# Feed-forward product stage: the activation remainders move from GpSimd to VectorE, the products are reordered, and split weights of three chunks are kept in DRAM

## The chip, the cores and the metric

The kernel runs on one core of a Trainium2 chip. The time is that of one execution in device microseconds (us). The engines are TensorE (PE: matmuls; PEld: its weight loads), VectorE (DVE), ScalarE (ACT), GpSimd (POOL) and the DMA queues, the main one of which is issued by SyncE (SP). Each engine works through its own instructions in the order of the program and waits for the others on semaphores.

## The reference

One step of a one-layer decoder: 2048 prompt tokens and 64 sample tokens of width 1024. The change touches only the second half of the feed-forward part:

```python
hid = jnp.square(jax.nn.relu(jnp.einsum('btd,df->btf', x, w_ff1)))     # 1024 -> 4096
x = _layer_norm(ALPHA * x + jnp.einsum('btf,fd->btd', hid, w_ff2), ln2_g, ln2_b)   # 4096 -> 1024
```

All is float32. The kernel gets near that accuracy from fp32r matmuls: each operand is cut in two, a rounded part and the remainder, and three products are summed (rounded x rounded, rounded x remainder, remainder x rounded).

## The kernel before

The prompt is worked on in four blocks of 512 tokens; block two (`b == 1`, the source counts from 0) also carries the 64 sample rows. Each block has four stages: the mixer (projections, recurrence, convolution), the output projection with layer norm, `ff1` (32 feature tiles against `w_ff1`) and `ff2`. The texts below number the blocks one to four.

**ff2.** The 4096 hidden features are eight chunks of 512 features (`NCH`; in block four the eighth chunk is worked off apart, after the other seven). For each chunk, tokens, features and output columns are halved, and a Strassen-like scheme does seven products in place of eight. A product (`step`) runs over all chunks before the next begins, so a block has 7 x 8 = 56 units, numbered here n = 0 to 55. A unit is 12 matmuls of 128x512 (L236 to L238). In block two the units of four of the steps (B11, B21, T1 and B22, the names in `SAMPLE`) carry four more, for the sample rows. A unit needs one weight tile of 128x1024 and one hidden tile of 128x512, each in two parts:

- the weight: SP loads it into one of three `st` buffers (L173); ACT rounds it into `wh` (L194); DVE subtracts and writes the remainder `wl` (L201). There are four `wh` and four `wl`. The call `weights(i)` prepares the unit three ahead, so `wh` of unit n+3 is written when TensorE has finished unit n-1. The steps T1 to T4 use sums of weight quarters, which DMAs of the POOL queue put together in DRAM in block one (`make_sums`).
- the hidden tile: `prepare` (L1033) works two units ahead. ACT rounds into `h` (L1040), and GpSimd writes the remainder `l` (L1041); three buffers each. Three of the steps also need a difference of hidden quarters, on DVE, in place (L1045, L1047, L1049); these were done at once, a unit after the use of the quarter that they overwrite, eight in a row.

**The products' banks.** Each product adds into two of the PSUM tiles named A to D (`PRODUCTS`). When its last chunk is done, DVE adds the two banks into the token rows `x1` (L1069, L1072: two instructions a destination, for T3 four); at the four sample steps it adds sample rows too (`sample_sums`, two or four instructions).

**Order on DVE.** What must wait for ACT is put into the list `later` and issued by the next `flush`, which `weights` calls first. So the program order on DVE after the last unit of a product is: the bank additions, then the weight remainder of the unit three ahead, then what `prepare` and the others left.

**The next block's input** comes as four tiles of transposed tokens (five for block two), put among the weights at `X_PLACES` and split in the same way. `tok` is a ring of eight 128x1024 tiles; four (five in block two) hold the rows `x1`.

Of the kernel before, what the change touches and what calls it, by code (L numbers as in the profile page):

```python
# [9 lines left out]
F32 = mybir.dt.float32  # L10
# [25 lines left out]
RAW = {"B11": 0, "B21": 1, "B12": 2, "B22": 3}  # L36
SUMS = ("T1", "T2", "T3", "T4")

PRODUCTS = (("B21", "C"), ("B11", "A"), ("T4", "D"), ("T2", "A"), ("T1", "B"), ("B22", "B"), ("T3", "A"))

SLOT_OF = {"B21": 3, "B11": 1, "T4": 2, "T2": 2, "T1": 1, "B22": 3, "T3": 0}

# [3 lines left out]

SAMPLE = {"B21": (1, ((0, 1),)), "B11": (0, ((0, 1), (1, -1))), "T1": (0, ((1, 1),)), "B22": (1, ((1, 1),))}

X_PLACES = (("B21", 2), ("B21", 5), ("B11", 2), ("B11", 5), ("B22", 5))
M_ORDER = (4, 5, 6, 7, 0, 1, 2, 3)  # L50


# [1 line left out]
def hybrid_step(ctx, tc, a, o):  # L54
# [10 lines left out]
    def new(shape, tag, bufs, dt=F32, of=None):  # L65
        count[0] += 1
        return (of or pool).tile(list(shape), dt, tag=tag, bufs=bufs, name=f"{tag}{count[0]}")
# [19 lines left out]
    def TOK(dt=F32):  # L87
        return new((P, D), "tok", 8, dt)
# [76 lines left out]

    def unit_dma():
        src, _, cols, _, _ = units[at["dma"]]
        st = TOK() if at["dma"] < 6 else new((P, D), "st", 3)
        if at["dma"] < 2:
            for half in (slice(0, D // 2), slice(D // 2, D)):  # L170
                nc.sync.dma_start(st[:, half], src[:, half])
        else:
            nc.sync.dma_start(st[:, :cols], src)  # L173
        stages[at["dma"]] = st
        at["dma"] += 1

    def unit_split():
        i = at["split"]
        at["split"] += 1
        _, scale, _, use, spare = units[i]  # L180
        st = stages.pop(i)
        if use is not None:
            use(st)
            return
        wh = new((P, D), "wh", 4, F32R)
        if i == 0:
            wl = new((P, D), "wl", 4, F32R)
            for half in (slice(0, D // 2), slice(D // 2, D)):
                split(wh[:, half], wl[:, half], st[:, half])
                flush()  # L190
            handles[i] = (wh, wl)
            return
        if scale is None:
            s.activation(wh, st, AF.Copy)  # L194
        else:
            s.activation(wh, st, AF.Identity, scale=scale)

        def low():
            wl = TOK(F32R) if spare else new((P, D), "wl", 4, F32R)
            if scale is None:  # L200
                v.tensor_tensor(wl, st, wh.bitcast(F32), ALU.subtract)  # L201
            else:
                v.scalar_tensor_tensor(wl, st, scale, wh.bitcast(F32), ALU.mult, ALU.subtract)
            handles[i] = (wh, wl)

        later.append(low)
# [10 lines left out]
    def weights(i, kept=0):  # L217

        ahead(i + 4 - kept)
        return handles.pop(i)  # L220
# [100 lines left out]
    def make_sums():  # L321
        def at(c, k):
            return a["w_ff2"][c * 4 + RAW[k]] if k in RAW else sums[c][k]

        for to, of, acc in (("T1", "B11", False), ("T3", "B22", False), ("T1", "B12", True), ("T3", "B12", True),
                            ("T2", "T3", False), ("T2", "B11", True), ("T4", "T2", False), ("T4", "B21", True)):
            for c in range(NCH):
                if acc:
                    g.dma_start(at(c, to), at(c, of), accum_op=ALU.add, max_dma_last_dim=4096)
                else:  # L330
                    g.dma_start(at(c, to), at(c, of), max_dma_last_dim=4096)
                yield

    making = make_sums()

    for b in range(NB):
        pl = {}
        pl["m1"] = [w_in(0)]
        if b == 0:
            for src, cols, use in x_units(0):  # L340
                add_unit(src, cols=cols, use=use)
        pl["m1"] += [w_in(i) for i in (4, 1, 5, 2, 6, 3, 7)]
        pl["m2"] = [w_in(20 + i) for i in range(8)]
        pl["m3"] = [[w_in(8 + 3 * ct + j) for j in range(3)] for ct in range(4)]
        pl["tiles"] = [[0, 1], [2, 3, 4] if b == SB else [2, 3]]

        pl["m4"] = [[(m, add_unit(a["w_out"][m], scale=onorm[:, m:m + 1] if m < 4 else None)) for m in ms]
                    for ms in (M_ORDER, M_ORDER[:-2])]
        nf = 8
        pl["f0"] = [[(f, add_unit(a["w_ff1"][f])) for f in fs] for fs in (range(nf), range(nf - 2))]  # L350
        pl["ff1"] = [(f, add_unit(a["w_ff1"][f])) for f in range(nf, NF)]
        pl["ff2"] = []
        pl["nc"] = NCH - 1 if b == NB - 1 else NCH
        nx = x_units(b + 1) if b + 1 < NB else []
        for step, _ in PRODUCTS:
            for c in range(pl["nc"]):
                pl["ff2"].append((step, c, add_unit(a["w_ff2"][c * 4 + RAW[step]] if step in RAW else sums[c][step])))
                if (step, c) in X_PLACES and nx:
                    src, cols, use = nx.pop(0)
                    add_unit(src, cols=cols, use=use)  # L360
        pl["last"] = [add_unit(a["w_ff2"][(NCH - 1) * 4 + k], spare=k == 3) for k in range(4)] if b == NB - 1 else []
        for src, cols, use in nx:
            add_unit(src, cols=cols, use=use)
        plan.append(pl)
# [7 lines left out]
    for b in range(NB):  # L372
# [451 lines left out]

        for i, _ in enumerate(main()):
            rec_step()
            if b == 0 and i >= 4:
                next(making, 0)
                next(making, 0)
            if i >= 16 and i % (3 if samp else 4) == 0:  # L830
                rec_step()
            if i % 2 == 0:
                pump()
# [199 lines left out]
        def prepare():  # L1033
            if not queue:
                return
            step, c = queue.pop(0)
            r = raw[c]
            x = r[:, SLOT_OF[step]]
            h, l = F((P, 2, 256), "h", 3, F32R), F((P, 2, 256), "l", 3, F32R)
            s.activation(h, x, AF.Copy)  # L1040
            g.tensor_tensor(l, x, h.bitcast(F32), ALU.subtract)  # L1041
            hid[step, c] = (h, l)

            if step == "T4":
                later.append(lambda: v.scalar_tensor_tensor(x, r[:, 0], -1.0, x, ALU.mult, ALU.subtract))  # L1045
            elif step == "T2":
                later.append(lambda: v.scalar_tensor_tensor(r[:, 1], x, -1.0, r[:, 1], ALU.mult, ALU.subtract))  # L1047
            elif step == "T1":
                later.append(lambda: v.scalar_tensor_tensor(r[:, 3], r[:, 2], -1.0, r[:, 3], ALU.mult, ALU.subtract))  # L1049
            elif step == "T3":  # L1050
                del raw[c]

        for i, (f, u) in enumerate(pl["ff1"]):
            if i >= len(pl["ff1"]) - 2:
                prepare()
            ff1(f, weights(u), segs)
        drain()
        norm_weights(1)
        if b == 0:
            for _ in making:  # L1060
                pass

        touched = set()

# [31 lines left out]
        to = dict(PRODUCTS)  # L1096
        banks = {}
        sample_rows()
        for step, c, u in pl["ff2"]:
            w = weights(u)  # L1100
            parts = [tuple(x[:, q * 512:q * 512 + 512] for x in w) for q in range(2)]
            prepare()
            if step in SAMPLE:
                sample_rows()
            if step == "T3" and pl["last"] and 2 <= c < 6:
                if c == 2:
                    last = [F((P, 4, 2, 256), "raw", NCH, F32R) for _ in range(2)]
                split(last[0][:, c - 2], last[1][:, c - 2], raw[NCH - 1][:, c - 2])
            k = to[step]
            first = k not in banks  # L1110
            if first:
                banks[k] = [PS() for _ in range(2)]
            h, l = hid.pop((step, c))
            for p in range(2):
                cs = slice(p * P, p * P + P)
                for q, (rh, rl) in enumerate(parts):
                    mm3_on(banks[k][p], h[:, q, cs], l[:, q, cs], rh, rl, first and q == 0, c == ncs - 1 and q == 1)
            if samp and step in SAMPLE:
                if c == 0:
                    ys = PS()  # L1120
                hp = spairs.pop(0)
                for q, (rh, rl) in enumerate(parts):
                    mm_pair(ys, hp[:, q, :], rh, rl, c == 0 and q == 0, c == ncs - 1 and q == 1)
            if c == ncs - 1:
                for t0, dh, sign in INTO[k][step]:
                    for p in range(2):
                        add_to(t0 + p, dh, banks[k][p], sign)
                if samp and step in SAMPLE:
                    sample_sums(ys, SAMPLE[step][1])
# [138 lines left out]
```

## Time and profile before

| | us |
|---|---|
| three timed runs | 2446.64, 2449.08, 2449.68 (median 2449.08) |
| profiled execution: its time | 2449.19 |
| profiled execution: its span, first to last instruction | 2447.4 |
| DVE busy / ACT busy / POOL busy | 1542.2 / 1114.9 / 524.9 |
| mean granted TensorE clock | 0.996 |

In the windows of the profile, "busy" of PE counts a matmul from its start to its modelled end; a matmul of 128x512 lasts 0.39 us but the next can start 0.227 us after it, so a busy PE can still be slower than it could be. In the rows of the waits, the three numbers are the sum in us, the count and the longest.

### The profile page before, as it was taken

The numbers are of one execution on the slowest core, as the hardware profiler recorded it, in microseconds if no ns is written. First come the engines' busy times: TensorE is split into PE (matmuls) and PEld (weight loads), VectorE is DVE, ScalarE is ACT, GpSimd is POOL, SyncE is SP. The second block draws the span as 40 slices with busy tenths as digits, with TensorE's granted clock in tenths as the row PEclk, the third lists the DMA queues.
The fourth block names the chain that finished last, engine by engine and source line by source line (L and its number), as shares of the span: only waits on it lengthen the run. The fifth ranks groups of instructions, "written<-read, shape, count | busy, mean of one in ns | idle before, by whom it ended". The sixth has DMA issues, their size and how long they took to land. (4 is left out here: it accounts for less than half of the span.)

```text
span 2447.4 us, 32997 instructions
## 1 busy us (share of the span) xinstructions
PE 2400.3 (98%) x12876; PEld 2051.5 (84%) x12876; DVE 1542.2 (63%) x2153; ACT 1114.9 (46%) x1794; POOL 524.9 (21%) x376
## 2 busy tenths in 40 slices
PE   7999999999999999999999999999999999999998
PEld 5888988878889889998778888988878888988876
DVE  5756822696865684227968857623886865822597
ACT  4334534654324354445554244534654334543553
POOL 3210000654001110004750000001662001000554
PEclk9999999999999999999999999999999999999999
DMA  9985423655223633225543225423654324433453
GB/s 329 277 233 174 160 97 112 199 186 179 79 78 75 211 121 104 87 96 164 180 149 118 91 80 190 144 96 129 206 188 146 104 82 159 161 103 116 163 184 113
DMA packets 103548, 358.79 MB, mean 147 GB/s; under 512 B 11552, under 2 KB 16032, under 8 KB 103392
## 3 DMA queue, kind: packets, MB, share of 16 engines
q1 hardware_dynamic: 91216, 313.88, 38.6%
q0 software_dynamic: 12032, 42.54, 6.5%
q8 instruction: 101, 1.65, 0.3%
q14 instruction: 55, 0.45, 0.1%
q10 hardware_dynamic: 144, 0.26, 0.0%
HBM read 345.59 MB, written 44.60 MB: 159 GB/s over the span
## 5 line engine op out<-in xcount | busy, mean ns | idle before, releaser
L201 DVE TENSOR_TENSOR wl<-st,wh 128x1024 fp32r<-128x1024 f32 x514 | 679.5, 1325 | 548.3 <-ACT wh L194 547.5
L230 PE MATMUL ps<-X,wh 128*128 128x512 f32 (+2 forms) x2272 | 779.6, 343 | 14.2 <-ACT X L155 11.0
L232 PE MATMUL ps<-X,wl 128*128 128x512 f32 (+2 forms) x2272 | 769.4, 339 | 1.0 <-DVE wl L201 1.0
L231 PE MATMUL ps<-X,wh 128*128 128x512 f32 (+2 forms) x2272 | 769.4, 339 | 0.5 <-DVE X L156 0.5
L194 ACT ACTIVATE wh<-st 128x1024 fp32r<-128x1024 f32 x515 | 543.1, 1055 | 381.0 <-DMA st<-T 90.8
L1041 POOL TENSOR_TENSOR l<-raw,h 128x512 fp32r<-128x512 f32 x217 | 391.6, 1808 | 947.3 <-ACT h L1040 930.9
L230 PEld LDWEIGHTS ps<-X,wh 128*128 128x128 f32 x2272 | 431.6, 190 | 60.6 <-ACT X L155 13.0
L232 PEld LDWEIGHTS ps<-X,wl 128*128 128x128 f32 x2272 | 431.3, 190 | 43.7 <-DVE wl L201 1.9
L231 PEld LDWEIGHTS ps<-X,wh 128*128 128x128 f32 x2272 | 431.7, 190 | 42.1 <-DVE X L156 2.6
L238 PE MATMUL ps<-wh,l 128*128 128x512 f32 x868 | 342.1, 394 | 8.9 <-POOL l L1041 8.9
L236 PE MATMUL ps<-wh,h 128*128 128x512 f32 x868 | 339.1, 391 | 6.3 <-DVE tok L1072 5.0
L237 PE MATMUL ps<-wl,h 128*128 128x512 f32 x868 | 339.2, 391 | 1.6 <-DVE wl L201 1.6
L1008 ACT ACTIVATE raw<-ps 128x256 f32<-128x256 f32 (+1 forms) x184 | 85.7, 466 | 372.6 <-PE ps L232 370.9
L238 PEld LDWEIGHTS ps<-wh,l 128*128 128x128 f32 x868 | 163.3, 188 | 53.1 <-POOL l L1041 19.9
L236 PEld LDWEIGHTS ps<-wh,h 128*128 128x128 f32 x868 | 163.4, 188 | 40.7 <-issue 6.2
L237 PEld LDWEIGHTS ps<-wl,h 128*128 128x128 f32 x868 | 163.2, 188 | 37.4 <-DVE wl L201 3.3
L1040 ACT ACTIVATE h<-raw 128x512 fp32r<-128x512 f32 x217 | 133.5, 615 | 7.7 <-PE ps L237 5.7
L262 POOL TENSOR_TENSOR sm<-sm,nhalf 128x1 f32<-128x1 f32 (+1 forms) x34 | 36.5, 1075 | 383.4 <-DVE sm L261 383.4
L230 PE MATMUL ps<-wh,X 128*128 128x512 f32 x256 | 104.0, 406 | 0.0
L230 PE MATMUL ps<-wh,S 128*128 128x512 f32 x256 | 101.3, 396 | 0.0
L232 PE MATMUL ps<-wh,X 128*128 128x512 f32 x256 | 100.3, 392 | 0.0
L232 PE MATMUL ps<-wh,S 128*128 128x512 f32 x256 | 99.9, 390 | 0.0
(204 smaller groups left out, 2560.4 us busy)
## 6 DMA issues: line engine op xcount, KB each, us to landing
st<-in_w_ff SPq DMA_DIRECT2D x249, 512.0 KB, 3.3
st<-T SPq DMA_DIRECT2D x124, 512.0 KB, 3.3
st<-in_w_in SPq DMA_DIRECT2D x110, 512.0 KB, 3.3
st<-in_w_out SPq DMA_DIRECT2D x56, 512.0 KB, 4.3
T<-in_w_ff POOLq DMA_DIRECT2D x48, 512.0 KB, 19.7
T<-T POOLq DMA_DIRECT2D x16, 512.0 KB, 17.8
lnb<-in_lnb SPq DMA_DIRECT2D x16, 512.0 KB, 5.9
tok<-in_x SPq DMA_DIRECT2D x16, 512.0 KB, 6.9
```

What stands on the lines that cost most here:

```text
L194: s.activation(wh, st, AF.Copy)
L201: v.tensor_tensor(wl, st, wh.bitcast(F32), ALU.subtract)
L230: te.matmul(out, lh, rh, start=first, stop=False)
L231: te.matmul(out, lh, rl, start=False, stop=False)
L232: te.matmul(out, ll, rh, start=False, stop=last)
L236: te.matmul(out, lh, rh, start=first, stop=False, skip_group_check=True)
L237: te.matmul(out, lh, rl, start=False, stop=False, skip_group_check=True)
L238: te.matmul(out, ll, rh, start=False, stop=last, skip_group_check=True)
L262: g.tensor_tensor(st[:n, 15:16], st[:n, 14:15], nhalf[:n, 0:1], ALU.pow)
L1008: s.activation(r[:, h0:h1], ps[:, :256 * (h1 - h0)].rearrange("p (s t) -> p s t", t=256), AF.Relu)
L1040: s.activation(h, x, AF.Copy)
L1041: g.tensor_tensor(l, x, h.bitcast(F32), ALU.subtract)
```

## The change

Six edits go together:

1. `prepare` calls `split`: the remainder `l` is a VectorE subtraction, put into `later`, in place of a GpSimd one issued at once.
2. The products run in the order T4, B11, B21, T2, T1, T3, B22. Their banks are then D, A, C, A, B, A, B; before they were C, A, D, A, B, B, A.
3. The differences of hidden quarters are no longer tied to `prepare`: `sum_rows` hands out one at a time, two in three units, from n = 3 to n = 37.
4. The tiles of the next block's input move from B21 and B11 (the first 16 units) to T3 and B22 (the last 16).
5. While `ff1` of block one runs, `keep_parts` makes the two parts of the weights of chunks 1, 4 and 6 for all seven steps: 21 tiles are loaded by SP, rounded by ACT, subtracted by DVE and stored as two tiles each by the POOL queue (42 stores). From block two on, those 3 of 8 units load both parts from DRAM straight into `wh` and `wl`; they have no `st` buffer, no rounding and no subtraction.
6. `make_sums` starts four steps later in the program and is finished ahead of `ff1`.

```diff
-PRODUCTS = (("B21", "C"), ("B11", "A"), ("T4", "D"), ("T2", "A"), ("T1", "B"), ("B22", "B"), ("T3", "A"))
+PRODUCTS = (("T4", "D"), ("B11", "A"), ("B21", "C"), ("T2", "A"), ("T1", "B"), ("T3", "A"), ("B22", "B"))
...
-X_PLACES = (("B21", 2), ("B21", 5), ("B11", 2), ("B11", 5), ("B22", 5))
+X_PLACES = (("T3", 0), ("T3", 4), ("B22", 0), ("B22", 3), ("B22", 5))
+KEPT = (1, 4, 6)
...
     def unit_dma():
         src, _, cols, _, _ = units[at["dma"]]
+        if isinstance(src, tuple):
+            at["dma"] += 1
+            return
...
     def unit_split():
...
+        if isinstance(src, tuple):
+            handles[i] = new((P, D), "wh", 4, F32R), new((P, D), "wl", 4, F32R)
+            for x, y in zip(handles[i], src):
+                nc.sync.dma_start(x.bitcast(F32), y)
+            return
...
+    def keep_parts():
+        last = None
+        for k, c in parts2:
+            t = TOK()
+            nc.sync.dma_start(t, quarter2(c, k))
+            if last:
+                last()
+            def done(t=t, to=parts2[k, c]):
+                h = TOK(F32R)
+                s.activation(h, t, AF.Copy)
+                def low():
+                    v.tensor_tensor(t.bitcast(F32R), t, h.bitcast(F32), ALU.subtract)
+                    g.dma_start(to[0], h.bitcast(F32))
+                    g.dma_start(to[1], t)
+                later.append(low)
+            last = done
+            yield
+        last()
...
-            if b == 0 and i >= 4:
+            if b == 0 and i >= 8:
                 next(making, 0)
...
-            s.activation(h, x, AF.Copy)
-            g.tensor_tensor(l, x, h.bitcast(F32), ALU.subtract)
+            split(h, l, x)
...
+        sumq = [(k, c) for k in ("T2", "T1", "B22") for c in range(ncs)]
+        def sum_rows():
...
+            later.append(lambda: v.scalar_tensor_tensor(r[:, to], r[:, of], -1.0, r[:, less], ALU.mult, ALU.subtract))
...
             ff1(f, weights(u), segs)
+            if b == 0:
+                next(keeping, 0)
...
-        for step, c, u in pl["ff2"]:
+        for n_, (step, c, u) in enumerate(pl["ff2"]):
             w = weights(u)
+            while (len(summed) * 3 + 6) // 2 <= n_ and sumq:
+                sum_rows()
...
             prepare()
```

On VectorE, at the end of the second product of block one, the rows were these (`tok` here are the token rows `x1`, `ps` the banks, `raw` the hidden quarters):

```order
L201 TENSOR_TENSOR wl_3899<-st_3879,wh_3881 128x1024
L1045 SCALAR_TENSOR_TENSOR raw_2149<-raw_2149 128x512
L1069 TENSOR_TENSOR tok_1929<-tok_1929,ps_3744 128x512
L1069 TENSOR_TENSOR tok_1931<-tok_1931,ps_3745 128x512
L201 TENSOR_TENSOR wl_3924<-st_3902,wh_3904 128x1024
L1045 SCALAR_TENSOR_TENSOR raw_2311<-raw_2311 128x512
L201 TENSOR_TENSOR wl_3949<-st_3927,wh_3929 128x1024
```

At the end of the first product of block one, VectorE's rows of the changed kernel are these (L1124 are the bank additions, L211 the weight remainders, L1101 the differences of hidden quarters, L158 the hidden remainders):

```order
L158 TENSOR_TENSOR l_3875<-raw_2191,h_3874 128x512
L1124 SCALAR_TENSOR_TENSOR tok_1818<-tok_1818,ps_3741 128x512
L1124 SCALAR_TENSOR_TENSOR tok_1820<-tok_1820,ps_3742 128x512
L211 TENSOR_TENSOR wl_3914<-st_3893,wh_3895 128x1024
L1101 SCALAR_TENSOR_TENSOR raw_2934<-raw_2934 128x512
L158 TENSOR_TENSOR l_3898<-raw_2353,h_3897 128x512
L211 TENSOR_TENSOR wl_3939<-st_3918,wh_3920 128x1024
```

The hidden remainder of the second unit after the product's end (`l_3898`) now stands on VectorE behind the two bank additions, the weight remainder and a difference of quarters; before, it stood on GpSimd, behind none of them.

In block two, at the end of B11, which is followed by B21, another step with sample rows, VectorE's rows of the changed kernel are these (L1135 and L1136 are the sample rows' additions, `hp` is the split sample part of the next unit):

```order
L1124 SCALAR_TENSOR_TENSOR tok_7613<-tok_7613,ps_10183 128x512
L1124 SCALAR_TENSOR_TENSOR tok_7615<-tok_7615,ps_10184 128x512
L1135 SCALAR_TENSOR_TENSOR tok_7617<-tok_7617,ps_10197 64x512
L1136 TENSOR_TENSOR tok_7617<-tok_7617,h_10405 64x512
L1135 SCALAR_TENSOR_TENSOR tok_7617<-tok_7617,ps_10197 64x512
L1136 TENSOR_TENSOR tok_7617<-tok_7617,h_10405 64x512
L211 TENSOR_TENSOR wl_10411<-st_10378,wh_10380 128x1024
L1101 SCALAR_TENSOR_TENSOR raw_7879<-raw_7879 128x512
L158 TENSOR_TENSOR l_10383<-raw_8049,h_10382 128x512
L158 TENSOR_TENSOR hp_10385<-tok_7867,hp_10385 128x2x64
```

Before, B11 was followed by T4, which has no sample rows, so that nothing waited for `hp` there, and `l` was not in the row; now the first unit of B21 waits for the tenth of these instructions.

In `ff1` of block one, ScalarE's rows of the changed kernel are these (L362 is the rounding of a kept weight, L204 that of an `ff1` weight, L1049 and L1051 are relu and square):

```order
L362 ACTIVATE tok_3004<-tok_2962 128x1024
L204 ACTIVATE wh_3013<-st_3011 128x1024
L1049 ACTIVATE raw_2934<-ps_3015 128x2x256
L1051 ACTIVATE raw_2934<-raw_2934 128x2x256
L362 ACTIVATE tok_3044<-tok_3002 128x1024
```

One rounding of a kept weight has been put behind the relu and square of each `ff1` unit. All of them write the same one of the eight `tok` buffers, so each waits until the store of the one before has landed.

More of the change, by code (lines that the diff above doesn't have):

```diff
@@ L179, in unit_split @@
         at["split"] += 1
-        _, scale, _, use, spare = units[i]
+        src, scale, _, use, spare = units[i]
+        if isinstance(src, tuple):
[3 more added lines that the diff above has]
+            return
         st = stages.pop(i)
@@ L334, in hybrid_step, with quarter2 @@
     making = make_sums()
+    parts2 = {(k, c): tuple(scratch.tile([P, D], F32, tag=f"{k}_{c}{x}", bufs=1, name=f"{k}_{c}{x}") for x in "hl")
+              for k in SLOT_OF for c in KEPT}
+    def quarter2(c, k):
+        return a["w_ff2"][c * 4 + RAW[k]] if k in RAW else sums[c][k]
+    def keep_parts():
[16 more added lines that the diff above has]
+        last()
+    keeping = keep_parts()
     for b in range(NB):
@@ L356, in hybrid_step @@
             for c in range(pl["nc"]):
-                pl["ff2"].append((step, c, add_unit(a["w_ff2"][c * 4 + RAW[step]] if step in RAW else sums[c][step])))
+                pl["ff2"].append((step, c, add_unit(parts2[step, c] if b > 0 and c in KEPT else quarter2(c, step))))
                 if (step, c) in X_PLACES and nx:
@@ L1039, in prepare @@
             h, l = F((P, 2, 256), "h", 3, F32R), F((P, 2, 256), "l", 3, F32R)
-            s.activation(h, x, AF.Copy)
-            g.tensor_tensor(l, x, h.bitcast(F32), ALU.subtract)
+            split(h, l, x)
             hid[step, c] = (h, l)
[L1044 to L1050, printed above, removed]
-                del raw[c]
+            if step in ("T2", "T1", "B22"):
+                assert (step, c) in summed
+            seen.add((step, c))
+            if step == "B22":
+                del raw[c]
+        sumq = [(k, c) for k in ("T2", "T1", "B22") for c in range(ncs)]
+        summed, seen = set(), set()
+        def sum_rows():
+            if not sumq:
+                return
+            k, c = sumq.pop(0)
+            assert (dict(T2="T4", T1="B11", B22="B21")[k], c) in seen
+            summed.add((k, c))
+            r = raw[c]
+            to, of, less = {"T2": (2, 0, 2), "T1": (1, 2, 1), "B22": (3, 2, 3)}[k]
+            later.append(lambda: v.scalar_tensor_tensor(r[:, to], r[:, of], -1.0, r[:, less], ALU.mult, ALU.subtract))
+        if b == 0:
+            for _ in making:
+                pass
         for i, (f, u) in enumerate(pl["ff1"]):
@@ L1056, in hybrid_step @@
             ff1(f, weights(u), segs)
+            if b == 0:
+                next(keeping, 0)
         drain()
         norm_weights(1)
-        if b == 0:
-            for _ in making:
-                pass
         touched = set()
@@ L1098, in hybrid_step @@
         sample_rows()
-        for step, c, u in pl["ff2"]:
+        if b == 0:
+            for _ in keeping:
+                pass
+        for n_, (step, c, u) in enumerate(pl["ff2"]):
             w = weights(u)
+            while (len(summed) * 3 + 6) // 2 <= n_ and sumq:
+                sum_rows()
             parts = [tuple(x[:, q * 512:q * 512 + 512] for x in w) for q in range(2)]
@@ L1104, in hybrid_step @@
                 sample_rows()
-            if step == "T3" and pl["last"] and 2 <= c < 6:
+            if step == "B22" and pl["last"] and 2 <= c < 6:
                 if c == 2:
```

## Prediction

> **What bounds the kernel now.** I read the page's busy shares first, then the windows by stage, then TensorE's timeline and waits.
>
> In the windows the columns are the stretch, its length, the busy time of PE, PEld, DVE, ACT and POOL with their counts, the granted clock, the DMA share and GB/s.
>
> ```profile
> PE 2400.3 (98%) x12876; PEld 2051.5 (84%) x12876; DVE 1542.2 (63%) x2153; ACT 1114.9 (46%) x1794; POOL 524.9 (21%) x376
> ...
> 40.00:433.80 393.80, 393.80 (x2115) 335.56 (x2114) 219.69 (x364) 166.66 (x271) 41.99 (x51) 1.00 0.60 179
> 433.80:593.00 159.20, 155.49 (x675) 125.14 (x675) 127.29 (x100) 93.78 (x120) 92.64 (x54) 1.00 0.62 200
> 1097.00:1289.00 192.00, 185.47 (x806) 149.26 (x806) 149.14 (x139) 102.48 (x156) 109.18 (x54) 1.00 0.50 164
> 1701.00:1862.00 161.00, 154.66 (x674) 125.71 (x673) 125.02 (x96) 92.52 (x116) 97.62 (x54) 1.00 0.60 196
> 2274.00:2414.00 140.00, 136.69 (x592) 111.51 (x592) 108.36 (x86) 79.62 (x102) 81.83 (x47) 0.99 0.55 181
> ```
>
> The kernel is bound by TensorE: busy for 98% of the span, and for all of the 393.8 us ahead of the first `ff2`. Nothing in the change alters its matmuls. What can be won lies in the four `ff2` stages, the last four rows, and the next rows say how much:
>
> ```profile
> 433.85 0.39 PE L236 MATMUL ps<-wh,h 128*128 128x512 f32 x1
> 434.07 0.39 PE L237 MATMUL ps<-wl,h 128*128 128x512 f32 x1
> 434.30 0.39 PE L238 MATMUL ps<-wh,l 128*128 128x512 f32 x1
> 434.52 0.39 PE L236 MATMUL ps<-wh,h 128*128 128x512 f32 x1
> ```
>
> A matmul lasts 0.39 us, but the next starts 0.227 us after it; a unit of 12 takes 2.72 us. At that pace the stages need 675 x 0.227 = 153.2, 806 x 0.227 = 183.0, 153.0 and 134.4 us. They took 159.2, 192.0, 161.0 and 140.0. So 6.0, 9.0, 8.0 and 5.6 us are lost, **28.6 us in all**: the most that this change can win.
>
> ```profile
> PE ps L238 <- POOL l L1041: 8.9, 11, 1.4
> PE ps L236 <- DVE tok L1072: 5.0, 3, 2.6
> PE ps L241 <- DVE hp L156: 3.1, 3, 1.3
> ```
>
> TensorE waits there for GpSimd's `l`, for bank additions (the step B22 adds into the banks that T1 has just left, and must wait until DVE has read them) and for the sample part. Each such wait costs 0.16 us more than its row says, because the row counts from the modelled end.
>
> **The removed parts.** Why `l` is late:
>
> ```profile
> L1041 POOL TENSOR_TENSOR l<-raw,h x217: 1287/1812/4113, 425.0 to 2407.5; 128x512 fp32r<-128x512 f32 x109
> ...
> 1776.77 0.68 DVE L1047 SCALAR_TENSOR_TENSOR raw<-raw 128x512 f32<-128x512 f32 x1
> 1777.37 1.21 DVE L201 TENSOR_TENSOR wl<-st,wh 128x1024 fp32r<-128x1024 f32 x1
> 1778.51 1.78 DVE L1047 SCALAR_TENSOR_TENSOR raw<-raw 128x512 f32<-128x512 f32 x1
> ...
> 1777.93 1.80 POOL L1041 TENSOR_TENSOR l<-raw,h 128x512 fp32r<-128x512 f32 x1 [2.17 <-ACT h L1040]
> ```
>
> The first row gives the shortest, the median and the longest: GpSimd takes 1.29 us at best and 1.81 in the median. DVE's difference takes 0.68 us alone and 1.78 where it falls on GpSimd's `l` (last row). Without GpSimd this stretching goes on both sides, the adjacent use of one bank goes with the new order, and the differences are spread. I cost all 28.6 us as gone and now add what the new order costs.
>
> **The added part: `l` behind the bank additions.** The prices on DVE, and for the weights' round, ACT's rounding and a load's time to landing:
>
> ```profile
> 1746.64 1.28 DVE L1069 TENSOR_TENSOR tok<-tok,ps 128x512 f32<-128x512 f32 x2
> L156 DVE TENSOR_TENSOR X<-S,X 128x512 fp32r<-128x512 f32 x16 | 11.0, 684 | 0.0
> L1084 DVE TENSOR_TENSOR tok<-tok,h 64x512 f32<-64x512 f32 x5 | 3.4, 684 | 0.2
> L156 DVE TENSOR_TENSOR hp<-tok,hp 128x128 fp32r<-128x128 f32 x32 | 27.9, 872 | 5.7 <-ACT hp L155 5.7
> ...
> L194 ACT ACTIVATE wh<-st 128x1024 fp32r<-128x1024 f32 x515 | 543.1, 1055 | 381.0 <-DMA st<-T 90.8 <-PE ps L238 83.5 <-PE ps L232 65.4
> st<-T SPq DMA_DIRECT2D x124, 512.0 KB, 3.3
> ```
>
> Followed directly by another, an instruction of 128x512 takes 0.60 us (1776.77 to 1777.37; two additions 1.28 = 0.60 + 0.68) and a weight remainder 1.14 (1777.37 to 1778.51). `l` of VectorE is priced by the 0.684 row. After the last matmul of a product the additions start about 0.25 us after the slot's end (0.39 - 0.227, and some 0.09 for the semaphore). `l` of the second unit on is read by that unit's third matmul, 2.72 + 0.45 = 3.17 us after the product's end. Behind two additions, a weight remainder and a difference it is ready at 0.25 + 1.20 + 1.14 + 0.60 + 0.68 = 3.87: **0.7 us of stall**; without a difference 0.1. After T3, with four additions and no difference: 4.47, so 1.3; where a kept weight leaves out the remainder, 0.16.
>
> - Block one: differences stand at n = 7, 15 and 31, not at 23, 39: 3 x 0.7 + 2 x 0.1 + 1.3 = 3.6. Here DVE does everything: 56 x (1.14 + 0.60) + 24 x 0.60 + 4 x 1.14 + 16 x 0.60 = 126 of 152 us. The input tiles now fall into the last 16 units, which must bring 21 tiles through three `st` buffers. A buffer's round was 3.3 us of DMA, 1.06 of rounding and 1.2 of remainder, 5.6 us for three, 1.9 each; with `l` of 0.6 and two hand-overs nearer 2.3, against 43.5 / 21 = 2.07 there. 21 x 0.23 is 5, the three-unit lead of `wh` absorbs up to all: 0 to 5, I take 2. Together 5.6.
> - Block two: after B11, DVE does two additions, four sample additions, remainder, difference, `l` and `hp` before the next unit's sample matmul, due 2.72 us on: 0.25 + 6 x 0.60 + 1.14 + 0.60 + 0.60 + 0.3 (between nothing and the row's 0.87) = 6.5, **a stall of 3.8 us**. After B21, two sample additions, no difference: 4.47 - 3.17 = 1.3. After T1, with a kept weight: 0.16. After T4, T2 and T3 the next unit has 16 matmuls and the stall is nothing. To this comes the clock, next.
> - Block three: 3 x 0.7 + 0.1 + 0.16 = 2.4. Block four: 3 x 0.7 + 2 x 0.1 + 1.3 = 3.6.
>
> ```profile
> 2371.03 0.40 PE L238 MATMUL ps<-wh,l 128*128 128x512 f32 x1
> 2374.03 0.47 PE L236 MATMUL ps<-wh,h 128*128 128x512 f32 x1 [2.60 <-DVE tok L1072]
> ...
> 2374.90:2378.30 3.40, 3.40 (x10) 2.62 (x9) 2.93 (x2) 0.42 (x1) 1.35 (x1) 0.50 0.74 275
> ```
>
> After an idle time of 2.60 us the granted clock is 0.50 for 3.4 us, which costs 1.7 us more. I put that 1.7 on the stall after B11: block two 7.0. The Trainium skill ("TensorE: Matmul & The Clock Gate", Part 1) has the clock halve only after an idle window of about 3.4 us that runs freely; by it a 3.8 us gap would seldom fill one, and the sum would be 1.7 us shorter. The drop after 2.60 us speaks against the rule.
>
> **The added part: 21 kept tiles in `ff1` of block one.**
>
> ```profile
> 380.00:400.00 20.00, 20.00 (x90) 16.57 (x89) 5.50 (x5) 8.36 (x12) 0.00 (x0) 1.00 0.25 84
> 10.00:20.00 10.00, 8.96 (x23) 4.92 (x21) 4.58 (x7) 3.98 (x8) 2.23 (x5) 1.00 1.03 415
> out_y<-tok POOLq DMA_DIRECT2D x12, 512.0 KB, 3.0
> ```
>
> A unit of `ff1` is 24 matmuls, 5.45 us. ACT is busy 8.36 of 20 us, DVE 5.5; a rounding (1.06) and a subtraction (1.2) per unit fit. The DMAs grow from one tile of 0.524 MB to four: 2.10 MB in 5.45 us, 385 GB/s. The second row shows 415 GB/s moved at a full share, so it fits, barely. All kept roundings share one buffer: rounding 1.06, two hand-overs (some 0.3), the store's landing, then the next. Up to a landing of 4.1 us that keeps the 5.45 us pace; alone it is 3.0. Past that ACT falls behind, and TensorE has the three units ahead in `wh`, 16 us less a rounding and a remainder, 14, before it notices. I take 0, with 0 to 26 as bounds (below).
>
> **Kept weights, blocks two to four.** Two loads start when TensorE leaves the buffer three units ahead, 8.2 us; two of 3.3 us one after the other are 6.6. SP waits in front of them, and the `st` loads queued behind it have a lead of their own of three units: 0. The traffic is 1.375 times the 196 GB/s of block three, 270. `make_sums`: GpSimd has nothing ahead of it, so its later place in the program changes no time. The end of the kernel has two bank additions in place of four: 0.
>
> **Sum.** 5.6 + 7.0 + 2.4 + 3.6 = 18.6 in place of 28.6: 10 us less. The profiled execution took 2449.19, its span 2447.4, the median of the runs is 2449.08, so they agree: **2439 us**.
>
> **Rivals.**
> - *The stalls vanish.* Between the products DVE runs ahead, and its instructions need less than the sums above. For it: nothing but the additions waits for TensorE. Against it: `l` stands behind them in program order. With 3 to 5 us left in all: 2424.
> - *Block one is bound by DVE and the `st` round.* It has 126 us of 152 on DVE with no kept weights, and its last third is 21 tiles in 43.5 us. If all 5 us and further 5 by lateness that hands itself on are lost: 2447, no change. For it: the roundings of `wh` already waited 90.8 us in all for `st<-T`.
> - *Slower: the one rounding buffer in `ff1`.* If the store's landing under 385 GB/s takes 6.0 us, twice the 3.0 (as if another transfer always shared the engines), a step takes 1.06 + 0.3 + 6.0 = 7.36 us; 21 x 1.91 = 40 us of lag, less 14 of cover: 26 us of stalls, 2465 with the gain of 10 elsewhere kept. It decides from a landing of 4.8 us on (21 x 0.67 = 14). For it: in the windows `ff2` moved 200 GB/s at a share of 0.62, which is only 322 at a full one. Against it: 415 in the other row, and the store is the first of its unit to be issued. The Trainium skill ("DMA: Bandwidth & Descriptors", Where 436 GB/s comes from) puts HBM to SBUF at about 358 GB/s for a core; by that a step would take 5.86 us and the lag of 8.6 us would stay under the cover. The 415 GB/s row, part of it copies inside DRAM, does not agree.
>
> **How the numbers follow.** A difference under 0.2% (5 us) can't be told from none. Forecast (2434 to 2444): 0.48. Stalls vanish (2422 to 2434): 0.20. Block one (2444 to 2454): 0.19. Slower, `ff1` (over 2454): 0.13. So faster 0.68, same 0.19, slower 0.13. The range 2424 to 2453 leaves out the slower case and the best few microseconds.
>
> **What would show it.** Right: no GpSimd subtraction; DVE's 128x512 at 0.68 throughout; TensorE's longest wait in `ff2` of block two, for `hp` after B11, some 3.6 us, with a granted clock of 0.5 after it; waits of 0.5 to 1.3 us for `l` at the ends of products and few elsewhere; `ff1` of block one gapless. Wrong: gaps there behind ACT; `wh` or `wl` of kept units waiting for DMAs; block one longer than 159 us.

## Result and profile after

| | median of the runs, us | lowest to highest | ratio to before, 95% interval |
|---|---|---|---|
| before | 2448.94 | 2446.64 to 2449.68 | |
| changed | 2506.94 | 2502.84 to 2508.29 | 1.0236 [1.0218, 1.0253] |

The change makes the kernel 58 us slower; 2439 was forecast, and the range ended at 2453. The profiled execution took 2508.29 us, its span 2506.5.

Windows by stage of the changed kernel (up to the first `ff2`, then the four `ff2` stages; columns as in the prediction's windows):

```profile
40.00:459.20 419.20, 401.84 (x2119) 335.76 (x2117) 241.74 (x383) 186.05 (x290) 61.99 (x91) 1.00 0.77 240
459.20:617.90 158.70, 157.51 (x673) 127.49 (x674) 131.05 (x159) 96.12 (x123) 0.73 (x2) 0.98 0.67 214
1121.10:1324.00 202.90, 190.28 (x802) 152.92 (x802) 115.60 (x173) 80.31 (x134) 0.00 (x0) 0.97 0.57 210
1736.40:1907.40 171.00, 158.59 (x674) 124.56 (x673) 103.13 (x132) 70.17 (x96) 0.00 (x0) 1.00 0.68 247
2319.80:2472.80 153.00, 140.49 (x590) 108.48 (x589) 86.53 (x115) 57.63 (x82) 0.00 (x0) 1.00 0.65 237
```

The first row was 393.80 us long with TensorE busy throughout; now it is 419.20 long and by its busy time TensorE is idle for 17 of them. The second is as it was. The last three have grown from some 192, 161 and 140 us, although DVE and ACT have less to do in them: DVE is busy 115.60 us in block two, where it was 149.14. DVE and ACT are emptier and the stages longer, so TensorE's stalls come from something other than their load.

The lengths from the first matmul of one stage to the first of the next, for all the runs that the reading rests on (the stretches ahead of the other three `ff2` stages agree within 1.7 us everywhere). The stages have 672, 800, 672 and 588 matmuls; the prediction's windows held a few of their neighbours, which made block two's pace 183.0:

| us | ahead of `ff2`, block one | `ff2` one | two | three | four |
|---|---|---|---|---|---|
| matmuls of the stage x 0.227 | | 152.5 | 181.6 | 152.5 | 133.5 |
| before | 425.4 | 158.9 | 191.4 | 160.8 | 139.3 |
| changed | 449.8 | 158.7 | 202.9 | 171.0 | 153.0 |
| e1, no kept weights | 424.6 | 154.5 | 190.8 | 156.0 | 134.8 |
| e2, made but not loaded | 443.1 | 158.0 | 189.0 | 155.9 | 134.9 |
| e3, loaded by GpSimd's queue | 450.0 | 158.3 | 187.6 | 154.6 | 135.7 |
| e5, made with buffers of their own | 423.8 | 155.2 | 189.2 | 155.3 | 134.9 |
| e8, e1 with the additions last | 425.3 | 152.3 | 181.6 | 152.3 | 133.3 |
| e11, both faults mended, additions last | 424.1 | 152.3 | 181.6 | 159.9 | 133.4 |

**Block one.** TensorE is not gapless in `ff1`. ScalarE's waits in the changed kernel between 325 and 459 us (sum, count, longest), then the spread of the kept roundings over the whole run and the time to landing of one of their stores:

```profile
ACT wh L204 <- DMA st<-in_w_ff: 27.1, 10, 4.5
ACT tok L362 <- DMA T_4h<-tok: 8.8, 2, 4.6
ACT tok L362 <- DMA T_1h<-tok: 8.7, 4, 5.1
...
L362 ACT ACTIVATE tok<-tok x21: 1040/1060/1062, 316.2 to 457.5; 128x1024 fp32r<-128x1024 f32 x21
...
T_4h<-tok POOLq DMA_DIRECT2D x4, 512.0 KB, 6.1
```

The 21 roundings start over 141.3 us, one every 141.3 / 20 = 7.07 us, where a unit of `ff1` has 5.45. None may start before the store of the rounding before has landed, which took 6.1 us for these tiles; 16 of the 21 waited for that, 40.8 us in all, and the other five did not. That is the prediction's rival "slower", which decides from a landing of 4.8 us on: 7.36 us a step and 26 us lost were worked out there, 7.07 and 24.4 measured (449.8 - 425.4).

There is a second wait, which the rival does not have: the first row above, 27.1 us for `st`, the weights of `ff1` itself. They stand on SP's queue, each behind the load of the next kept tile (L356), and that load waits for a `tok` buffer until the store of an earlier remainder has landed. Two pairs on SP's queue, ScalarE's wait for the second of the two `st` loads, and the longest sum of SP's waits between 325 and 459 us (all six rows of this kind make 111.1):

```profile
375.05 0.33 SPq L356 DMA_DIRECT2D tok<-T  x1
375.47 0.38 SPq L178 DMA_DIRECT2D st<-in_w_ff  x1
383.27 0.33 SPq L356 DMA_DIRECT2D tok<-T  x1
383.69 0.40 SPq L178 DMA_DIRECT2D st<-in_w_ff  x1
```
```profile
390.83 1.06 ACT L204 ACTIVATE wh<-st 128x1024 fp32r<-128x1024 f32 x1 [4.33 <-DMA st<-in_w_ff]
```
```profile
SPq L356 <- DMA B_4l<-tok: 23.4, 3, 9.3
```

**Blocks two to four.** The queue of SP in the changed kernel, in block three (start, time to issue, what it loads), and ScalarE at the same place:

```profile
1779.83 0.86 SPq L178 DMA_DIRECT2D st<-in_w_ff  x2
1788.47 0.33 SPq L189 DMA_DIRECT2D wh<-B_4h  x1
1788.85 0.42 SPq L189 DMA_DIRECT2D wl<-B_4l  x1
1789.33 0.42 SPq L178 DMA_DIRECT2D st<-in_w_ff  x1
1794.83 0.32 SPq L189 DMA_DIRECT2D wh<-B_6h  x1
1795.19 0.43 SPq L189 DMA_DIRECT2D wl<-B_6l  x1
1795.72 0.38 SPq L178 DMA_DIRECT2D st<-in_w_ff  x1
```
```profile
1801.58 1.06 ACT L204 ACTIVATE wh<-st 128x1024 fp32r<-128x1024 f32 x1 [4.30 <-DMA st<-in_w_ff]
1802.55 0.61 ACT L157 ACTIVATE h<-raw 128x512 fp32r<-128x512 f32 x1
```

From 1780.69 to 1788.47 SP issues nothing: the kept load of B_4 waits for TensorE to leave a `wh` buffer. The `st` load behind it needs no such buffer, but it goes only at 1789.33, and the next only after B_6, at 1795.72. ScalarE waits for that load until 1801.58, 4.30 us, and the rounding `h` behind it waits too. The waits of the whole run, SP's first:

```profile
SPq L189 <- PE ps L248: 290.5, 49, 12.9
...
PE ps L248 <- DVE l L158: 25.6, 32, 1.9
PE ps L246 <- ACT h L157: 10.2, 13, 4.1
PE ps L251 <- DVE hp L158: 6.0, 5, 4.6
```

TensorE's own waits name `l` and `h`, not a DMA, so the table of its waits alone points to VectorE. The queue's waits, two steps further back, name another cause, which e3 below tests. The time to landing of `st<-T`, 3.3 us before, is now this:

```profile
st<-T SPq DMA_DIRECT2D x88, 512.0 KB, 5.8
```

### The profile page after: what moved, and what is told of

It is laid out like the page before. It is cut to its first block, busy times and chain, and to the rows that moved or that the text cites. A ratio compares the mean times of both kernels' runs of the same rounds, so it can differ in the third digit from the quotient of the medians.

```text
span 2506.5 us, 33068 instructions
## 1 busy us (share of the span) xinstructions
PE 2421.2 (97%) x12876; PEld 2052.8 (82%) x12876; DVE 1485.7 (59%) x2328; ACT 1067.1 (43%) x1752; POOL 153.8 (6%) x201
## 4 chain that ended last, share of the span: by engine, by line
PE 77%; issue 8%; DMA 8%; DVE 4%; ACT 2%; POOL 1%; SPq 1%; DVEq 0%; POOLq 0%; ACTq 0%
PE ps L240 18%; PE ps L242 18%; PE ps L241 18%; PE ps L248 5%; PE ps L246 5%; PE ps L247 5%; DMA st<-T 4%; PE ps L692 2%; DMA st<-in_w_ff 2%; ACT wh L204 1%; DVE l L158 1%; DVE wl L211 1%; PE ps L251 1%; PE ps L252 1%; DMA st<-in_w_in 1%
## 5 line engine op out<-in xcount | busy, mean ns | idle before, releaser
L211 DVE TENSOR_TENSOR wl<-st,wh 128x1024 fp32r<-128x1024 f32 x451 | 550.9, 1222 | 554.9 <-ACT wh L204 553.6
L204 ACT ACTIVATE wh<-st 128x1024 fp32r<-128x1024 f32 x452 | 476.0, 1053 | 505.4 <-DMA st<-T 134.4
L248 PE MATMUL ps<-wh,l 128*128 128x512 f32 x868 | 345.9, 399 | 26.0 <-DVE l L158 25.6
L1049 ACT ACTIVATE raw<-ps 128x256 f32<-128x256 f32 (+1 forms) x184 | 85.3, 464 | 308.8 <-PE ps L242 306.9
L158 DVE TENSOR_TENSOR l<-raw,h 128x512 fp32r<-128x512 f32 x217 | 146.9, 684 | 27.7 <-ACT h L157 27.7
```

Of the source, the lines that this page charges most:

```text
L158: later.append(lambda: v.tensor_tensor(lo, src, hi.bitcast(F32), ALU.subtract))
L248: te.matmul(out, ll, rh, start=False, stop=last, skip_group_check=True)
L1049: s.activation(r[:, h0:h1], ps[:, :256 * (h1 - h0)].rearrange("p (s t) -> p s t", t=256), AF.Relu)
```

## Experiments

Three theories stood at the start. A: the kept weights cost the time, by two waits, the one rounding buffer in block one and the loads that wait at the head of SP's queue. B: `l` behind the bank additions on VectorE costs it. C: the transfers themselves are too many. Later A's first half was split into A1 (the one buffer) and A2 (the transfers). The ratios are to the kernel before as measured beside each group: 2447.30 us for e1 to e4, 2449.18 for e5 to e8, 2448.48 for e9 to e12, 2448.84 for e13 and e14. Where a cut of the source leaves lines out, three dots stand.

**e1: no kept weights, everything else as changed.**

```diff
-KEPT = (1, 4, 6)
+KEPT = ()
...
```

> The changed kernel (2507 us) without kept weights: nothing is made in ff1 of block one, and every block rounds and subtracts all its weights; the new order, the spread differences and the remainder on VectorE stay. Theory A (the kept weights cost the time at both ends: some 25 us where they are made in ff1, and 35 to 39 us in ff2 of blocks two to four, where their loads hold up SyncE's queue): 2444 us, and ff2 of block three as long as that of block one, 159 us. Rival B (the loss in ff2 comes from the remainder standing on VectorE behind the bank additions): only the 25 us of ff1 go, 2482 us.

Measured: 2432.04 us, ratio 0.9935 [0.9919, 0.9952]. The kept weights cost 75 us, and the rest of the change wins 15. That is 12 us below what A expected, 2444, which put the cost of the kept weights at some 63. B falls: `l` stands behind the additions here too, and TensorE waits for it 2.8 us in all:

```profile
PE ps L251 <- DVE hp L158: 3.4, 1, 3.4
...
PE ps L248 <- DVE l L158: 2.8, 6, 0.7
```

**e2: parts made and stored, never loaded.**

```diff
-                pl["ff2"].append((step, c, add_unit(parts2[step, c] if b > 0 and c in KEPT else quarter2(c, step))))
+                pl["ff2"].append((step, c, add_unit(quarter2(c, step))))
```

> The changed kernel makes and stores the kept parts, but every block goes on loading the whole weights, so nothing reads what was stored. Theory A: ff2 of blocks two to four gets back its 35 to 39 us, ff1 of block one stays long: 2470 us. If the two losses were one (lateness carried from ff1 onwards): 2507 us.

Measured: 2461.12, 1.0049 [1.0033, 1.0065]. Making costs 29 us (2461 - 2432), loading the other 46. The profiled execution took 2455.56, 23 us more than e1's; of these, 18.5 lie ahead of `ff2` of block one and 3.5 in it (443.1 and 158.0 against 424.6 and 154.5).

**e3: as changed, the kept loads issued by GpSimd's queue in place of SP's.**

```diff
-                nc.sync.dma_start(x.bitcast(F32), y)
+                g.dma_start(x.bitcast(F32), y)
```

> The changed kernel with the loads of kept parts issued by GpSimd's queue in place of SyncE's, so that no other load stands behind them. Theory A (head of the line on SyncE's queue): the waits of ff2 in blocks two to four go, 2470 us. Rival C (the DMA engines carry 1.375 times the bytes and are late with everything): 2500 us or more.

Measured: 2460.11, 1.0053 [1.0037, 1.0069]. The same bytes move, and all 46 us are back. The kept loads wait as long, 122.5 us in block three for 116.1 in the changed kernel, but on a queue where nothing that ScalarE needs stands behind them, and ScalarE's wait for `st` there falls from 61.5 us (41.0 + 20.5) to 4.1. The rows of `ff2` of block three, in the changed kernel (1736.4 to 1907.3 us) and in e3 (1722.2 to 1876.8 us):

```profile
SPq L189 <- PE ps L248: 116.1, 20, 10.8
ACT wh L204 <- DMA st<-T: 41.0, 9, 6.6
ACT wh L204 <- DMA st<-in_w_ff: 20.5, 6, 4.8
```
```profile
POOL wh L189 <- PE ps L248: 122.5, 19, 12.7
ACT wh L204 <- DMA st<-in_w_ff: 4.1, 2, 3.6
```

C falls for blocks two to four.

**e4: as changed, `l` back on GpSimd.**

```diff
-            split(h, l, x)
+            s.activation(h, x, AF.Copy)
+            g.tensor_tensor(l, x, h.bitcast(F32), ALU.subtract)
```

> The changed kernel with the remainder of the hidden tiles back on GpSimd, issued at once. Rival B (it stands behind the bank additions on VectorE): some 35 us less, 2472 us. Theory A: the kept weights' cost stays, and GpSimd stretches VectorE's instructions again: 2507 us, 10 more or less.

Measured: 2520.49, 1.0299 [1.0272, 1.0325], two runs. B would have made it faster; it is 14 us slower, and a little outside A's range too (2507, 10 more or less). TensorE waits for `l` 30.6 us here and 25.6 in the changed kernel. That GpSimd's longer subtraction comes on top of an `h` that is late already would explain it, but no run shows it apart.

**e5: as e2, but the rounded part goes into the hidden-tile buffers, idle in `ff1`: three instead of one.**

```diff
-                h = TOK(F32R)
-                s.activation(h, t, AF.Copy)
+                hs = [new((P, 2, 256), x, 3, F32R, phase["of"]).rearrange("p a b -> p (a b)") for x in "hl"]
+                for q, h in enumerate(hs):
+                    s.activation(h, t[:, q * 512:q * 512 + 512], AF.Copy)
...
```

> As the version that makes the parts and never loads them (2461), but the rounded part goes into three buffers of its own (the hidden-tile buffers, idle in ff1, two halves each) in place of the one shared one. The same bytes are moved. Theory A1 (one buffer: each rounding waits until the store of the one before has landed): the stretch ahead of ff2 of block one goes from 443 back to 425 to 430 us, time 2433 to 2440. Theory A2 (the transfers themselves: 21 x 4 tiles of 0.524 MB are 44 MB, 128 us at the 343 GB/s that 292 GB/s at a share of 0.85 comes to, where 21 units last 114): the stretch stays at 438 or more, time 2447 or more.

Measured: 2432.91, 0.9933 [0.9916, 0.9949]. The making costs 1 us instead of 29, with the same bytes. Windows of e5 and of the changed kernel, over their stretches of making (e5 is through at 433):

```profile
325.00:433.00 108.00, 108.00 (x479) 89.41 (x478) 53.41 (x65) 64.84 (x100) 30.67 (x57) 1.00 1.00 378
```
```profile
325.00:459.00 134.00, 116.78 (x484) 90.18 (x483) 46.98 (x43) 59.98 (x76) 19.26 (x37) 0.99 0.85 293
```

With the chain cut, the DMAs move 378 GB/s at a share of 1.00 and TensorE is busy for all 108 us. In the changed kernel they are idle for 0.15 of the time: the wait held back the transfers, not the other way round. The stores land no sooner in e5, 6.3 us for a half tile of `T_4h` and 8.3 for a whole one of `T_4l`; with three buffers no rounding waits for them. A2 falls. A1 holds in so far as buffers, and not bytes, were short. But the edit also takes the rounded parts out of `tok`, so the loaded tiles have its free buffers to themselves, and both waits of block one are eased together: SP still waits 77 us at L356 between 325 and 433 us, and ScalarE 23 us for `st`, now 3.5 at most, and 1 us is lost. What each of the two waits cost alone is not shown.

```profile
T_4l<-tok POOLq DMA_DIRECT2D x4, 512.0 KB, 8.3
...
T_4h<-h POOLq DMA_DIRECT2D x4, 256.0 KB, 6.3
```

**e6: as e2, without the 42 stores.** The two `g.dma_start` lines of `low` are left out, so nothing of the parts reaches DRAM.

> As the version that makes the parts and never loads them, without the 42 stores: the 21 loads, roundings and subtractions stay. A1 and A2 (both put the cost into the stores): stretch ahead of ff2 of block one 425 to 428, time 2432 to 2436. Rival A3 (ScalarE's and VectorE's added work holds up the ff1 weights): stretch 435 or more, time 2444 or more.

Measured: 2430.77, 0.9927 [0.9910, 0.9943]: 21 loads, roundings and subtractions beside `ff1` cost nothing that can be measured. That step of the prediction's working was right.

**e7: as e1, `l` back on GpSimd** (the edit of e4).

> No kept weights (2432), and l back on GpSimd: what stays of the change is the order of the products, the spread differences and the later input tiles. Theory E (the engine of l makes the 15 us gain): 2442 to 2450, near the kernel before, waits for POOL l back at 7 us or more. Theory O (order and spread make it): 2430 to 2437.

Measured: 2433.10, 0.9933 [0.9918, 0.9949], as e1. Theory E falls, that the engine of `l` makes e1's gain of 15 us: the move of `l` to VectorE, one of three things by which the prediction had the stalls go, wins nothing here. GpSimd's `l` is no shorter, 1.78 us in the median; it is less often the last thing (4.9 us of waits, before 8.9):

```profile
L1083 POOL TENSOR_TENSOR l<-raw,h x217: 1287/1781/4589, 424.8 to 2392.5; 128x512 fp32r<-128x512 f32 x109
...
PE ps L248 <- POOL l L1083: 4.9, 7, 1.5
```

**e9: as e1, the input tiles back among the first 16 units.**

```diff
-X_PLACES = (("T3", 0), ("T3", 4), ("B22", 0), ("B22", 3), ("B22", 5))
+X_PLACES = (("T4", 2), ("T4", 5), ("B11", 2), ("B11", 5), ("B22", 5))
```

> No kept weights (2432), with the next block's input tiles back among the first 16 units of ff2 (in T4 and B11), four of five. With l on GpSimd or on VectorE the time without kept weights was the same (2433, 2432), so the 15 us come from the order of the products, the spread differences or the later input tiles. If the later input tiles make them: 2440 or more, new waits in the first 16 units. If not: 2429 to 2435.

Measured: 2432.39, 0.9936 [0.9920, 0.9952]: no difference from e1.

**e12: as e1, the differences of hidden quarters back in rows of eight**, each behind the `l` of T4, T2 or T1 (the old lines of `prepare`).

> No kept weights (2432), with the differences of hidden quarters back in rows of eight, one behind each l of T4, T2 and T1, in place of two in three units. If the spreading makes the 15 us: 2440 or more. If the order of the products (no bank used by two products in a row) makes them: 2430 to 2436.

Measured: 2429.37, 0.9921 [0.9905, 0.9936]: no loss, if anything a little better than e1.

**e13: the kernel before with the new order of the products alone**, so none of these three edits and no kept weights.

```diff
-PRODUCTS = (("B21", "C"), ("B11", "A"), ("T4", "D"), ("T2", "A"), ("T1", "B"), ("B22", "B"), ("T3", "A"))
+PRODUCTS = (("T4", "D"), ("B11", "A"), ("B21", "C"), ("T2", "A"), ("T1", "B"), ("T3", "A"), ("B22", "B"))
...
```

The lines left out keep the input tiles at their old places in the stage, under the new names of the steps. `make_sums` is as in the kernel before, too.

> The kernel before (2449) with the new order of the products alone: l stays on GpSimd, differences in rows of eight, input tiles in the first 16 units, no kept weights. Each of the other three edits was undone singly without a loss (2433, 2432, 2429). If the order makes the 15 us: 2428 to 2436. If it needs one of the others (any one of them being enough): 2440 or more.

Measured: 2452.14, 1.0015 [1.0005, 1.0025]. A miss for the theory that the order makes the gain. Its own wait is gone: the bank wait, `tok L1072`, 5.0 us before, isn't among its waits any more. Others have come:

```profile
PE ps L238 <- POOL l L1041: 10.2, 11, 1.4
PE ps L241 <- DVE hp L156: 7.2, 4, 4.1
```

The order moves T4 to the front. There, by program order, its eight differences, the input tiles and GpSimd's `l` fall into the same first units: seven of e13's eight stalls over 0.25 us in `ff2` of block one lie in its first 52 us. With the order, taking any one of the three edits back left the gain standing (e7, e9, e12); with none of them there was none (e13). Which single one would be enough was not tried. The later `make_sums`, which e13 lacks as well, is no rival for blocks two and three: it works in block one alone, and those two blocks take 10.0 us longer in e13 than in e1.

**e8: as e1, the additions at a product's end issued last.**

```diff
             if c == ncs - 1:
-                for t0, dh, sign in INTO[k][step]:
...
-                    sample_sums(ys, SAMPLE[step][1])
+                def sums_(k=k, step=step, ys=ys if samp and step in SAMPLE else None):
+                    for t0, dh, sign in INTO[k][step]:
...
+                        sample_sums(ys, SAMPLE[step][1])
+                if n_ < len(pl["ff2"]) - 1:
+                    later.append(sums_)
+                else:
+                    sums_()
```

> No kept weights (2432), and the bank additions and sample additions at a product's end are put into the list of things issued later, behind the weight remainder, l and hp that are waiting there. If the waits left in ff2 (16 us by stage lengths, of which 3.5 for hp after B11 and up to 0.8 each for l) come from instructions that stand behind the additions: the stall for hp goes, few l waits above 0.3, time 2420 to 2428. If VectorE's total is what is short, or the reuse of a bank: new waits at the start of the next product, 2430 or more.

Measured: **2417.71, 0.9870 [0.9852, 0.9889]**, faster than both kernels and than was expected. `ff2` takes 152.3, 181.6, 152.3 and 133.3 us, the bare pace, and no wait of `ff2` is left among TensorE's; all those over 0.3 us belong to the other stages:

```profile
PE ps L240 <- ACT X L157: 12.7, 4, 9.8
PE ps L240 <- ACT wh L204: 3.8, 2, 2.5
PE ps L242 <- DVE wl L211: 0.7, 2, 0.5
PE ps L240 <- DVE S L613: 0.5, 1, 0.5
```

**e10: the kernel before with that edit alone.**

> The kernel before (2449), with one edit: the additions at a product's end are issued behind the waiting weight remainder and hp, as in the version that took 2418. If that place is all that the stalls of ff2 hang on: 2428 or less. If the adjacent use of one bank (T1 and then B22 into B, B22 waits until VectorE has read it) counts: that wait grows from 2.6 us by about a remainder each, and the time stays at 2440 to 2452.

Measured: 2450.07, 1.0013 [1.0003, 1.0023]. With the old order B22 adds into the bank that T1 has just left, and additions that come later make that wait longer, 12.4 us for 5.0:

```profile
PE ps L236 <- DVE tok L1072: 12.4, 4, 4.4
```

**e14: e13 with that edit.**

> The run above with the additions at a product's end issued last. If the place of the additions and the order of the products are the two things that the stalls of ff2 hang on: 2416 to 2422, though l is on GpSimd. If l on VectorE is needed as well once the additions are out of the way: waits for POOL l of 4 us or more in all, 2424 or more.

Measured: 2438.55, 0.9959 [0.9944, 0.9974]. It wins 14 us over e13 but lacks 21 to e8: order and additions are not all. TensorE waits 7.2 us for GpSimd's `l`, and stalls are still bunched in the first units; whether `l` on VectorE, the spread or the places would take them away was not tried one by one.

**e11: e8 with kept weights in which both faults are mended** (buffers of e5, loads of e3).

> The version that took 2418 with the kept weights put back in a form that mends both faults: rounded parts in three buffers of their own, and kept loads issued by GpSimd's queue. If kept weights cost only through those two faults: 2415 to 2422, no gain over 2418 because TensorE has no stall left in ff2 for them to take away. If two tiles per kept unit through the DMAs cost by themselves: 2425 or more. If they also shorten something outside ff2: below 2414.

Measured: 2421.81, 0.9891 [0.9873, 0.9909]. Even so the kept weights win nothing, and 4 us are lost. In the profiled execution, the slowest of four (2425.48), block three has 7.5 us of stalls, in part for the kept loads themselves:

```profile
PE ps L247 <- DMA wl<-B_4l: 2.0, 1, 2.0
PE ps L247 <- DMA wl<-T_4l: 1.7, 1, 1.7
```

The kept weights take work from ScalarE and VectorE, and in e8 neither holds up TensorE in `ff2`, so there is nothing to win.

## Why the prediction was wrong

- **Kept weights, blocks two to four: "SP waits in front of them, and the `st` loads queued behind it have a lead of their own of three units: 0".** This step failed, and there was no rival for it. The lead of `st` counts in program order; the queue issues in order too, so an `st` load behind a kept load starts only when TensorE has left the kept unit's buffer. Put at 0, it cost 12 + 15 + 18 = 45 us in the three stages, against e1. The working named what is queued behind the wait and then gave it a lead that the wait itself takes away. The other half was right: two loads of 3.2 and 4.2 us do fit under the 8.2 us of the buffers; no wait for them is among TensorE's in the changed kernel.
- **21 kept tiles in `ff1` of block one: "I take 0, with 0 to 26 as bounds".** The wrong end was taken. One mechanism, its point of decision and its price stood among the rivals (26 us; 24.4 measured), with a chance of 0.13. That the price fits so well is in part luck, because the second wait, the `st` loads behind held loads on SP's queue, was in no sum. The row chosen for the landing, 3.0 us, was of `out_y` stores, around which the DMAs' share was 0.24 to 0.39 (windows of the kernel before, 590 to 700, 1289 to 1330 and 1862 to 1900 us); at 0.85 it is 6.1. The argument against, that the bandwidth suffices, was true (378 GB/s in e5) and beside the point: bandwidth doesn't say how long one store takes. The Trainium skill's 358 GB/s ("DMA: Bandwidth & Descriptors", Where 436 GB/s comes from) does not agree with e5's 378 over 108 us, loads and stores together.
- **"I cost all 28.6 us as gone", then 18.6 back for `l` behind the additions.** Without the kept weights (e1) the sum was near: 2432 measured for 2439, and the new stalls come to 16.4 us (2.1, 9.3, 3.5, 1.5, from the starts of the matmuls) for 18.6 (5.6, 7.0, 2.4, 3.6). But it is near by luck, for its terms miss to both sides. With the stages' true numbers of matmuls the kernel before loses 30.3 us and not 28.6. The 0.7 us for `l` behind two additions and a difference, counted three times in each of blocks one, three and four, is 0.24 or 0.25 in e1 at each of these places (in block one the second units of B11, B21 and T1, which start at 458.04, 480.04 and 523.80 us). The 1.3 after T3 is 0.83 in blocks one and four. The stall after B11 in block two is 6.3 us for 5.5: the first matmul that needs `hp` came 3.51 us late (3.8 forecast), and those behind it lost 2.8 more (1.7 forecast), because the clock stayed low past the first 3.4 us:

```profile
1148.15 0.77 PE L251 MATMUL ps<-wh,hp 128*128 128x512 f32 x1 [3.35 <-DVE hp L158]
...
1148.20:1151.60 3.40, 3.40 (x8) 2.75 (x9) 3.05 (x5) 1.77 (x3) 0.00 (x0) 0.50 0.72 254
1152.00:1156.00 4.00, 4.00 (x15) 3.17 (x15) 0.93 (x3) 0.54 (x1) 0.00 (x0) 0.76 0.38 134
```

  That these stalls hang on the place of the additions is shown by e8, which moves them and has no stall left.
- **Why `l` was late.** The prediction put it down to GpSimd's duration. The duration is real, but with the new order, spread and places it costs nothing more than VectorE's (e7). The bunch of stalls in e13's first units suggests that several things falling together make them; no run shows that by itself.
- **The cover for block one, "2" us for the `st` round in the last 16 units.** e9, with four of the tiles at the old place, has 155.2 us in that stage and e1 154.5, so nothing is lost by the later place.
- **The check list.** As foretold: no GpSimd subtraction, and the `hp` wait in block two with a clock of 0.50 after it (4.6 us in the changed kernel, 3.6 forecast). Not as foretold: few waits for `l` away from the ends of products; the changed kernel has 32 of them over the whole run, up to 1.9 us. Of its three signs of failure one was seen, gaps in `ff1` behind ACT. Kept units waiting for DMAs were not seen (the units behind them waited), and block one's `ff2` was not longer.

## What to carry to other kernels

A load that waits for a buffer holds up every load behind it on its queue, so a lead counted in buffers is worth only what the instruction ahead of it on the queue leaves; put loads with long waits on a queue where nothing urgent stands behind them. A store that must land before its buffer is written again belongs in a chain with its landing time under load; here more buffers gave back what looked like a lack of bandwidth. And work that nobody waits for at once, here the additions at a product's end, goes behind the work that someone does wait for. That pays only where the next product leaves the bank alone: with the old order it won nothing (e10).

## What the runs showed of the hardware

The DMAs kept up 378 GB/s for 108 us at a share of 1.00 (e5), beside a gapless TensorE. In that time the stores landed late: 6.3 us for half a tile of `T_4h` and 8.3 for a whole tile of `T_4l` issued behind the halves, where a whole tile of `out_y` took 2.9 at another time of the same run. How much of this is the size and how much the queue is not shown.

The granted clock was low after a shorter wait than the prediction's 2.60 us, too. In the kernel before, ahead of `ff2` of block two, a wait of 1.67 us was followed by 3.4 us at 0.51, while after one of 1.44 us in block three (up to 1784.34 us) the clock stayed at 1.00. After e1's 3.35 us matmuls were still 0.43 us apart at 1153.84, 5.7 us later. The rows are of the kernel before:

```profile
913.57 0.42 PE L230 MATMUL ps<-X,wh 128*128 128x320 f32 x1 [1.67 <-ACT X L155]
...
913.90:917.30 3.40, 3.14 (x12) 3.05 (x12) 3.18 (x6) 1.10 (x3) 0.00 (x0) 0.51 0.14 57
```
